# A hybrid encoder block: the first modulation block cut to three k-tiles and summed by two engines

## The chip, the cores and the metric

One core of a Trainium2 chip. The metric is the time of one execution on the device, in microseconds; the number shown is the median of three runs.

## The reference

256 rows `x` of 2048 channels go through one layer. What matters here is its start:

- `mod = silu(c) @ ada_w + ada_b`, with `c` one vector of 2048 and `ada_w` 2048 x 12288, gives shift1, scale1, gate1, shift2, scale2 and gate2 (2048 each).
- `h = RMSNorm(x) * norm1_g * (1 + scale1) + shift1`
- `proj = h @ w_in` (2048 x 9216): columns for a gated MLP (u, v), for attention (q, k, v) and for two gates.

After that come the spatial gating, a banded attention, the merge through `w_out`, a second modulated norm, a router, 32 SwiGLU experts (top 2 of 8 in the best of 4 groups) and a final norm. All is float32.

## The kernel before, in words

A *k-tile* is 128 of the 2048 channels; there are 16. Shift1 and scale1 of a k-tile need 128 columns of two sixths of `ada_w`, over all 2048 rows: 2.1 MB. Only then can that k-tile of `h` be made, and used in products with `w_in`. The kernel therefore walks through `h` in blocks (`BLOCKS`, L40): four blocks of four k-tiles.

`ada_block(k0, n)` (L184) is a generator that does the modulation of one block. It loads 4 chunks of `16 // n` row tiles, each as two DMAs on SP (L192, shift columns and scale columns, 1 MB each), multiplies each row tile by its silu column and adds up on VectorE (L202 the first, L204 the others, 1024 elements wide), transposes the sums on TensorE (L214) and reduces them on VectorE (L217). Three small operations (L220 to L222) make shift and scale, ScalarE applies them (L227), and `h` is kept in two float32r parts, `hh` (L230) and `hl` (L231).

Ahead of the first block: SP issues the ada loads at once; ScalarE's queue issues the small row loads (L158) and the two halves of x (L161); ScalarE squares x (L248) and scales it (L251), TensorE transposes it (L256) and ScalarE copies it out (L261) as `hx`. The spatial weights are transposed there as well (L266).

`run_steps` (L273) does the products of one column group of 1024 with the k-tiles of one block. There are five groups of this kind (`homes`: q, k, v, then the two of the gated MLP), so a block of n k-tiles makes 5n steps. A load brings up to four k-tiles (L108, 2 MB). Per step, ScalarE makes the high half of the weights (L315), VectorE the low half (L316), into two buffers each, and TensorE does 12 products (L289, L290, L291: high by high, low by high, high by low). The products of a step are issued after the preparation of the next. At the end of a group ScalarE copies the result out in the first block (L348), and VectorE adds it in later ones (L350).

The order of the work: `run_steps` takes one item of the next block's `ada_block` after each load and one after each step (`with_ada`). An item is a chunk's pair of loads, one sum, or a piece of the end. All loads of w_in and of ada chunks share one ring of four 16 KB slots, `r0` to `r3` (L100), in the order of the program, and SP issues them in that order: a load waits until its slot's last tenant, four loads before, has been used up. For the last block and for later stages the other four parts of `mod` come the same way (`ada_units`, sums at L427).

```python
for b, n in enumerate(BLOCKS):
    nxt = ada if lastb else ada_block(k0 + n, BLOCKS[b + 1])
    for c0, dst, func in homes:
        run_steps(lh_h, ll_h, win, k0, n, c0, ..., with_ada=nxt, ...)
    ...
    for _ in nxt:
        pass
```

## Time and profile before

| what | value |
|---|---|
| time, median of 3 runs | 1701.71 us (1701.52 to 1702.71) |
| time of the profiled execution | 1703.12 us |
| its span | 1701.3 us, 18241 instructions |
| its mean granted TensorE clock | 0.964 |
| busy share: TensorE, VectorE, ScalarE, GpSimd | 91, 56, 28, 7% |
| mean DMA rate over the span | 368 GB/s |
| chain that ended last | PE 48%, DMA 44%, VectorE 5% |

The shares are averages over three stretches that differ: a front until the first product of `w_in`, a middle of projections and attention, and the experts. In the views, PE is TensorE, PEld its weight loads, DVE VectorE, ACT ScalarE, POOL GpSimd, SP the queue that issues most loads; L204 is line 204 of the kernel. A mean of a group is the time of one instruction; what stands after an arrow is what ended the idle time before it. PEclk is the granted clock as a share of the full one.

### The profile page before, as it was taken

What the parts mean: (1) busy time and instruction counts of PE and PEld (TensorE: products, weight loads), DVE (VectorE), ACT (ScalarE), POOL (GpSimd) and SP (SyncE); (2) the same over time, 40 slices, a digit from 0 to 9 for tenths busy, and PEclk for the clock granted to TensorE, in tenths of its full rate; (3) what the DMA queues carried; (4) which work ended last, traced back from release to release, by engine and by line L of the source; (5) the groups of instructions that cost most, each with busy time, mean ns of one, the idle gap of its engine ahead of it and who ended that gap; (6) DMA issues with size and microseconds to landing.
All of it is one profiled execution on the core that took longest, in us unless ns stands there. A gap on an engine that the chain in (4) does not pass through costs nothing.

```text
span 1701.3 us, 18241 instructions
## 1 busy us (share of the span) xinstructions
PE 1539.8 (91%) x6717; PEld 863.6 (51%) x6717; DVE 951.2 (56%) x1332; ACT 484.4 (28%) x793; POOL 127.2 (7%) x377
## 2 busy tenths in 40 slices
PE   2999999999999999799998989989889898988986
PEld 1777778777887776553333423334333243333332
DVE  5789999998778879733432333323333233332333
ACT  4554345675444345331110111101111011111112
POOL 1000000000000000011100101001010010100101
PEclk8999999999999999799999999999999999999998
DMA  9988997797987876889999999999999999999995
GB/s 359 341 316 332 346 342 298 287 339 285 356 315 295 338 297 235 340 325 418 416 418 418 416 418 415 419 417 417 419 415 418 417 417 418 415 418 417 417 418 196
DMA packets 136766, 625.25 MB, mean 368 GB/s; under 512 B 5592, under 2 KB 7760, under 8 KB 103264
## 3 DMA queue, kind: packets, MB, share of 16 engines
q1 hardware_dynamic: 134240, 614.49, 90.9%
q10 hardware_dynamic: 992, 5.28, 0.8%
q0 software_dynamic: 1440, 4.27, 0.8%
q8 instruction: 55, 0.90, 0.2%
q14 instruction: 39, 0.32, 0.0%
HBM read 621.91 MB, written 2.10 MB: 367 GB/s over the span
## 4 chain that ended last, share of the span: by engine, by line
PE 48%; DMA 44%; DVE 5%; ACT 1%; issue 1%; SPq 0%; POOL 0%; POOLq 0%; DVEq 0%; ACTq 0%
DMA r<-in_w_dram 22%; PE b L1211 11%; PE b L291 10%; PE b L289 10%; DMA E<-in_w_dram 10%; PE b L290 10%; DMA dC<-in_w_dram 10%; DMA r<-in_ada_w_dram 2%; PE b L1236 2%; DVE W L316 1%; PE b L1075 1%; DVE f L427 1%; DVE f L204 0%; PE b L1262 0%; ACT W L315 0%
## 5 line engine op out<-in xcount | busy, mean ns | idle before, releaser
L1264 DVE TENSOR_TENSOR dB<-dB,b 128x512 f32<-128x512 f32 x248 | 153.6, 681 | 326.8 <-PE b L1262 326.8
L315 ACT CAST W<-r 128x1024 fp32r<-128x1024 f32 (+1 forms) x224 | 220.8, 988 | 329.0 <-PE b L290 289.7
L1211 PE MATMUL b<-r,e 128*64 128x512 f32 x1024 | 260.7, 627 | 44.4 <-DMA r<-in_w_dram 44.4
L316 DVE TENSOR_TENSOR W<-r,W 128x1024 fp32r<-128x1024 f32 (+1 forms) x224 | 255.2, 1144 | 62.5 <-ACT W L315 61.3
L289 PE MATMUL b<-W,dC 128*128 128x512 f32 x704 | 284.7, 405 | 5.5 <-ACT dC L230 3.7
L290 PE MATMUL b<-W,dD 128*128 128x512 f32 x704 | 280.1, 398 | 0.0
L291 PE MATMUL b<-W,dC 128*128 128x512 f32 x704 | 267.3, 398 | 2.0 <-DVE W L316 1.9
L1254 ACT CAST f<-f 64x512 fp32r<-64x512 f32 x124 | 76.4, 616 | 590.4 <-DVE dB L1264 430.4
L1211 PEld LDWEIGHTS b<-r,e 128*64 128x64 f32 x1024 | 91.1, 144 | 203.3 <-issue 137.7
L427 DVE SCALAR_TENSOR_TENSOR f<-r,sc,f 128x1024 f32<-128x1024 f32 x123 | 157.3, 1279 | 4.6 <-DMA r<-in_ada_w_dram 3.8
L289 PEld LDWEIGHTS b<-W,dC 128*128 128x128 f32 x704 | 132.8, 189 | 41.1 <-ACT dC L230 4.1
L291 PEld LDWEIGHTS b<-W,dC 128*128 128x128 f32 x704 | 131.5, 188 | 38.6 <-DVE W L316 7.1
L290 PEld LDWEIGHTS b<-W,dD 128*128 128x128 f32 x704 | 132.8, 189 | 30.6 <-issue 0.5
L1211 PE MATMUL b<-E,e 128*64 128x512 f32 x256 | 124.1, 642 | 23.7 <-DMA E<-in_w_dram 23.7
L1211 PE MATMUL b<-dC,e 128*64 128x512 f32 x256 | 118.3, 617 | 19.0 <-DMA dC<-in_w_dram 19.0
L1227 DVE TENSOR_TENSOR f2y<-f2y,b 128x256 f32<-128x256 f32 x32 | 13.5, 422 | 210.2 <-ACT f2y L1226 210.2
L1211 PE MATMUL b<-dD,e 128*64 128x512 f32 x256 | 126.1, 643 | 0.2 <-DMA dD<-in_w_dram 0.2
L1211 PE MATMUL b<-W,e 128*64 128x512 f32 x256 | 120.1, 618 | 0.0
L1236 PE MATMUL b<-r,f2y 128*64 128x512 f32 (+1 forms) x528 | 115.5, 590 | 2.3 <-DVE f2y L1227 2.3
L1255 DVE TENSOR_TENSOR f<-f,f 64x512 fp32r<-64x512 f32 x124 | 85.1, 686 | 26.1 <-ACT f L1254 23.1
L1337 POOL COPY e<-a 128x64 f32 x256 | 69.1, 273 | 195.9 <-PE b L1211 194.4
L1211 PEld LDWEIGHTS b<-E,e 128*64 128x64 f32 x256 | 36.4, 147 | 88.0 <-issue 52.7
(297 smaller groups left out, 1515.8 us busy)
## 6 DMA issues: line engine op xcount, KB each, us to landing
r<-in_w_dram SPq DMA_DIRECT2D x93, 2048.0 KB, 28.1
r<-in_w_in_dram SPq DMA_DIRECT2D x36, 2048.0 KB, 9.2
r<-in_ada_w_dram SPq DMA_DIRECT2D x32, 2048.0 KB, 9.3
W<-in_w_dram SPq DMA_DIRECT2D x24, 2048.0 KB, 28.1
dC<-in_w_dram SPq DMA_DIRECT2D x24, 2048.0 KB, 28.2
dD<-in_w_dram SPq DMA_DIRECT2D x24, 2048.0 KB, 28.2
E<-in_w_dram SPq DMA_DIRECT2D x24, 2048.0 KB, 7.7
r<-in_ada_w_dram SPq DMA_DIRECT2D x32, 1024.0 KB, 10.3
```

The lines of the kernel that those rows point to most:

```text
L289: nc.tensor.matmul(o, a, wh[:, cs], start=(k == k0), stop=False)
L290: nc.tensor.matmul(o, b, wh[:, cs], start=False, stop=False)
L291: nc.tensor.matmul(o, a, wl[:, cs], start=False, stop=close)
L315: nc.scalar.copy(wh, src)
L316: nc.vector.tensor_sub(wl, src, wh.bitcast(F32))
L427: nc.vector.scalar_tensor_tensor(out=acc, in0=rw[:, jj, :], scalar=sc[:, j : j + 1], in1=acc, op0=ALU.mult, op1=ALU.add,)
L1211: nc.tensor.matmul(pab[a * CH : (a + 1) * CH, :], xe[:, 8 * half + j, :], w[:, j // JQ, j % JQ, :], start=(half == 0 and j == 0), stop=(ha ...
L1236: nc.tensor.matmul(po[a * CH : (a + 1) * CH, 0:cw], act[:, j, :], w[:, j, o : o + cw], start=(j == 0), stop=(j == 3),)
L1254: pin(nc.scalar.copy(oh[r, a, :], og[r, b, :]))
L1255: pin(nc.vector.tensor_sub(oh[o, a, :], og[r, b, :], oh[r, a, :].bitcast(F32)))
L1264: pin(nc.vector.tensor_add(xa[:, t, d0 : d0 + 512], xa[:, t, d0 : d0 + 512], pr))
L1337: nc.gpsimd.tensor_copy(xe[:, JQ * q + j, :], Xg[q][j][:, ds(o, CAP)])
```

## The change

- The blocks have 3, 5, 4 and 4 k-tiles.
- The first block has a function of its own, `ada_first`. Its chunks have 4 row tiles of 384 columns. The shift part is summed on TensorE: the silu columns, broadcast to 64 equal columns each, are the stationary operand, and even and odd row tiles go to the two halves of one PSUM bank. The scale part is summed on VectorE as before. Products with one column (`pick`, which takes one row of each half, and `ones`) turn both sums into columns. `hh` comes from one ScalarE operation out of `hx`, and VectorE makes the full value and `hl`.
- The block of five is done as two `ada_block`s of 3 and 2, in one chain, with 2.2 items instead of one at each turn (`hurried`). Chunks have 4 row tiles, or 8 where the block has two k-tiles.
- Both halves of x are issued first on ScalarE's queue; the row loads go to SP, ahead of the ada loads (two of ada_b become one), and `gmlp_b_s` to GpSimd's queue. x is scaled by VectorE; the copies of its transposes alternate between ScalarE and VectorE. The table for Silu is loaded by an early operation, and the squares are held behind the silu of c.
- The transposes of the spatial weights become a side job that runs between steps.

```diff
--- before.py
+++ after.py
@@ -37,7 +37,7 @@
 CW = 1024
 Q = 4
 JQ = D // (Q * P)
-BLOCKS = (4, 4, 4, 4)
+BLOCKS = (3, 5, 4, 4)
 PACE = (0.75, 1.0, 1.0, 0.8, 0.7, 0.7, 0.7)
 OUT_CUTS = ((0, 1024), (1024, 512), (1536, 512))
 
@@ -145,29 +145,31 @@
 
 
     xt = [T([P, D], f"x{t}") for t in range(NT)]
+    for t in range(NT):
+        nc.scalar.dma_start(out=xt[t], in_=x[0, t * P : (t + 1) * P, :])
     rows = T([P, P], "a2")
     nc.vector.memset(rows, 0.0)
     r0 = 0
-    for src in (
-        c[0].rearrange("(j p) -> j p", p=P),
-        norm1_g[0].rearrange("(j p) -> j p", p=P),
-        ada_b[0, 0:D].rearrange("(j p) -> j p", p=P),
-        ada_b[0, D : 2 * D].rearrange("(j p) -> j p", p=P),
-        gmlp_b_s[0],
+    for src, queue in (
+        (c[0].rearrange("(j p) -> j p", p=P), nc.sync),
+        (norm1_g[0].rearrange("(j p) -> j p", p=P), nc.sync),
+        (ada_b[0, 0 : 2 * D].rearrange("(j p) -> j p", p=P), nc.sync),
+        (gmlp_b_s[0], nc.gpsimd),
     ):
-        nc.scalar.dma_start(out=rows[r0 : r0 + src.shape[0], :], in_=src)
+        queue.dma_start(out=rows[r0 : r0 + src.shape[0], :], in_=src)
         r0 += src.shape[0]
-    for t in range(NT):
-        nc.scalar.dma_start(out=xt[t], in_=x[0, t * P : (t + 1) * P, :])
     ws = [T([P, 4, P], "a0"), T([P, 4, P], "a1")]
     for i in range(2):
         nc.gpsimd.dma_start(out=ws[i], in_=gmlp_w_s[0, 4 * i : 4 * i + 4].rearrange("g t s -> t g s"))
+
+    nc.scalar.activation(mhalf[:, 1:2], mhalf[:, 0:1], AF.Silu)
+    nc.vector.memset(mhalf[:, 1:2], -0.5)
     cps = bk.ps()
     nc.tensor.transpose(cps[:, 0:P], rows, ident)
     cols = T([P, P], "cols")
     nc.vector.tensor_copy(cols, cps[:, 0:P])
     sc = T([P, ND], "sc")
-    nc.scalar.activation(sc, cols[:, 0:ND], AF.Silu)
+    sc_made = nc.scalar.activation(sc, cols[:, 0:ND], AF.Silu)
     g1c = cols[:, 16:32]
     b_shift = cols[:, 32:48]
     b_scale = cols[:, 48:64]
@@ -181,11 +183,10 @@
     hl = T([P, ND, S], "dD", F32R)
     accs = Ring(["f0", "f4"])
 
-    def ada_block(k0, n):
+    def ada_pieces(k0, n):
 
         w = n * P
-        acc = accs.sb([P, 2, w])
-        nj = 16 // n
+        nj = 4 if n > 2 else 8
         for j0 in range(0, ND, nj):
             rw = raws.sb([P, nj, 2, w])
             for m in range(2):
@@ -195,6 +196,63 @@
                         0, j0 * P : (j0 + nj) * P, m * D + k0 * P : m * D + k0 * P + w
                     ].rearrange("(j p) n -> p j n", p=P),
                 )
+            yield j0, nj, rw
+
+    def modulation(ks, sums):
+        nc.vector.tensor_add(sh1[:, ks], sums[:, 0, :], b_shift[:, ks])
+        nc.vector.tensor_add(sg1[:, ks], sums[:, 1, :], b_scale[:, ks])
+        nc.vector.scalar_tensor_tensor(
+            out=sg1[:, ks], in0=sg1[:, ks], scalar=1.0, in1=g1c[:, ks], op0=ALU.add, op1=ALU.mult
+        )
+
+    def ada_first(n):
+
+
+        w = n * P
+        scb = T([P, ND, CH], "f4")
+        nc.vector.tensor_copy(scb, sc.unsqueeze(2).to_broadcast([P, ND, CH]))
+        pick = T([P, 1], "pick")
+        nc.vector.tensor_add(pick, ident[:, 0:1], ident[:, CH : CH + 1])
+        pacc = bk.ps()
+        part = T([P, 2, w], "f0")
+        for j0, nj, rw in ada_pieces(0, n):
+            for jj in range(nj):
+                j = j0 + jj
+                i = j % 2
+                nc.tensor.matmul(
+                    pacc[i * CH : (i + 1) * CH, 0:w], scb[:, j, :], rw[:, jj, 0, :],
+                    start=(j < 2), stop=(j >= ND - 2),
+                )
+                if j == 0:
+                    nc.vector.tensor_scalar(part[:, 1, :], rw[:, jj, 1, :], sc[:, 0:1], None, op0=ALU.mult)
+                else:
+                    nc.vector.scalar_tensor_tensor(
+                        out=part[:, 1, :], in0=rw[:, jj, 1, :], scalar=sc[:, j : j + 1], in1=part[:, 1, :],
+                        op0=ALU.mult, op1=ALU.add,
+                    )
+            yield
+        nc.scalar.copy(part[:, 0, :], pacc[:, 0:w])
+        tp = sk.ps()
+        for m, what in enumerate((pick, ones[:, 0:1])):
+            for i in range(n):
+                nc.tensor.matmul(
+                    tp[:, m * n + i : m * n + i + 1], part[:, m, i * P : (i + 1) * P], what,
+                    start=True, stop=True,
+                )
+        modulation(slice(0, n), tp[:, 0 : 2 * n].rearrange("p (a b) -> p a b", a=2))
+        for j in range(n):
+            s, b = sg1[:, j : j + 1], sh1[:, j : j + 1]
+            nc.scalar.activation(hh[:, j, :], hx[:, j, :], AF.Identity, bias=b, scale=s)
+            full = scr[:, j * S : (j + 1) * S]
+            nc.vector.tensor_scalar(full, hx[:, j, :], s, b, op0=ALU.mult, op1=ALU.add)
+            nc.vector.tensor_sub(hl[:, j, :], full, hh[:, j, :].bitcast(F32))
+        yield
+
+    def ada_block(k0, n):
+
+        w = n * P
+        acc = accs.sb([P, 2, w])
+        for j0, nj, rw in ada_pieces(k0, n):
             yield
             for jj in range(nj):
                 j = j0 + jj
@@ -217,11 +275,7 @@
             nc.vector.tensor_reduce(
                 out=sums[:, m, :], in_=tp[:, 0:w].rearrange("p (a b) -> p a b", a=n), axis=AX.X, op=ALU.add
             )
-        nc.vector.tensor_add(sh1[:, ks], sums[:, 0, :], b_shift[:, ks])
-        nc.vector.tensor_add(sg1[:, ks], sums[:, 1, :], b_scale[:, ks])
-        nc.vector.scalar_tensor_tensor(
-            out=sg1[:, ks], in0=sg1[:, ks], scalar=1.0, in1=g1c[:, ks], op0=ALU.add, op1=ALU.mult
-        )
+        modulation(ks, sums)
         yield
         for j in range(k0, k0 + n):
             nc.scalar.activation(
@@ -229,8 +283,24 @@
             )
             nc.scalar.copy(hh[:, j, :], hx[:, j, :])
             nc.vector.tensor_sub(hl[:, j, :], hx[:, j, :], hh[:, j, :].bitcast(F32))
-            if j % 2 == 1:
+            if (j - k0) % 2 == 1 or j == k0 + n - 1:
                 yield
+
+    def ada_of(k0, n):
+
+        if n <= 4:
+            return ada_block(k0, n)
+        return hurried(itertools.chain(ada_block(k0, 3), ada_block(k0 + 3, n - 3)), 2.2)
+
+    def hurried(g, rate):
+        due = 0.0
+        while True:
+            due += rate
+            while due >= 1.0:
+                due -= 1.0
+                if next(g, "end") == "end":
+                    return
+            yield
 
 
     def inv_rms(ss, name):
@@ -241,16 +311,19 @@
         nc.gpsimd.tensor_tensor(out=rs, in0=ve, in1=mhalf, op=ALU.pow)
         return rs
 
-    first = ada_block(0, BLOCKS[0])
+    first = ada_first(BLOCKS[0])
+    next(first)
     ss1 = T([P, NT], "ss1")
     scr = T([P, D], "e2")
-    for t in range(NT):
-        nc.scalar.activation(scr, xt[t], AF.Square, accum_out=ss1[:, t : t + 1])
+    with tc.issue_after(sc_made.ins):
+        for t in range(NT):
+            nc.scalar.activation(scr, xt[t], AF.Square, accum_out=ss1[:, t : t + 1])
     rs1 = inv_rms(ss1, "n1")
     for t in range(NT):
-        nc.scalar.activation(xt[t], xt[t], AF.Copy, scale=rs1[:, t : t + 1])
+        nc.vector.tensor_scalar(xt[t], xt[t], rs1[:, t : t + 1], None, op0=ALU.mult)
+    turned = Ring(["b2", "b3", "b4", "b5", "b6", "b0"])
     for j in range(0, ND, 2):
-        tp = bk.ps()
+        tp = turned.ps()
         for jj in range(2):
             for t in range(NT):
                 nc.tensor.transpose(
@@ -258,16 +331,26 @@
                     xt[t][:, (j + jj) * P : (j + jj + 1) * P],
                     ident,
                 )
-        nc.scalar.copy(hx[:, j : j + 2, :], tp.rearrange("p (a b) -> p a b", a=2))
-    wsT = T([P, 8, P], "f3")
-    for i in range(2):
-        tp = bk.ps()
-        for g in range(4):
-            nc.tensor.transpose(tp[:, g * P : (g + 1) * P], ws[i][:, g, :], ident)
-        nc.scalar.copy(wsT[:, 4 * i : 4 * i + 4, :], tp.rearrange("p (a b) -> p a b", a=4))
-    nc.gpsimd.memset(wsT[CH:P, :, 0:CH], 0.0)
+        tv = tp.rearrange("p (a b) -> p a b", a=2)
+        if j % 4 == 0:
+            nc.scalar.copy(hx[:, j : j + 2, :], tv)
+        else:
+            nc.vector.tensor_copy(hx[:, j : j + 2, :], tv)
     for _ in first:
         pass
+    wsT = T([P, 8, P], "f3")
+
+    def turn_ws():
+        for i in range(2):
+            tp = sk.ps()
+            for g in range(4):
+                nc.tensor.transpose(tp[:, g * P : (g + 1) * P], ws[i][:, g, :], ident)
+            nc.scalar.copy(wsT[:, 4 * i : 4 * i + 4, :], tp.rearrange("p (a b) -> p a b", a=4))
+            yield
+        nc.gpsimd.memset(wsT[CH:P, :, 0:CH], 0.0)
+        yield
+
+    sides.append(turn_ws())
 
 
     def run_steps(lh, ll, w, k0, n, c0, evac, with_ada=None, cw=CW, after=None):
@@ -489,7 +572,7 @@
     k0 = 0
     for b, n in enumerate(BLOCKS):
         lastb = b == len(BLOCKS) - 1
-        nxt = ada if lastb else ada_block(k0 + n, BLOCKS[b + 1])
+        nxt = ada if lastb else ada_of(k0 + n, BLOCKS[b + 1])
         if lastb:
             vecs = T([P, 2, 8, S], "dB")
             lngb = vecs[:, 0].rearrange("p (a b) c -> p a (b c)", a=2)
```

## Rows read from the trace of the kernel before

**Rows 1.** Busy time by stretch, after the count PEclk, DMA share and GB/s.

```profile
0.00:45.00 45.00, 9.27 (x50) 7.57 (x50) 24.69 (x33) 19.30 (x25) 6.91 (x13) 0.87 1.00 362
45.00:90.00 45.00, 45.00 (x182) 35.83 (x182) 34.83 (x33) 22.77 (x31) 0.00 (x0) 0.94 0.92 344
210.00:260.00 50.00, 48.09 (x214) 37.85 (x213) 48.18 (x58) 21.24 (x27) 3.53 (x5) 1.00 0.90 336
820.00:1690.00 870.00, 777.82 (x3308) 299.04 (x3304) 294.10 (x502) 116.39 (x253) 85.20 (x273) 0.96 1.00 409
```

**Rows 2.** Chain of waits, 0 to 46 us: start, duration, what.

```profile
0.77 0.45 SPq L192
...
18.34 14.52 DMA r<-in_ada_w_dram
...
36.94 1.30 DVE f L204
...
45.00 0.79 PE b L289
```

**Rows 3.** Waits of TensorE, 45 to 330 us: total, times, longest.

```profile
PE b L291 <- DVE W L316: 1.7, 3, 1.2
PE b L214 <- DVE f L204: 1.1, 1, 1.1
```

**Rows 4.** Timeline of TensorE and VectorE, 87 to 115 us: start, duration, what.

```profile
87.61 0.39 PE L289 MATMUL b<-W,dC 128*128 128x512 f32 x1
...
90.43 0.39 PE L289 MATMUL b<-W,dC 128*128 128x512 f32 x1
...
114.68 0.69 DVE L350 TENSOR_TENSOR E<-E,b 128x512 f32<-128x512 f32 x1 [1.43 <-PE b L291]
```

**Rows 5.** Timeline of the front, the way of x.

```profile
20.75 3.90 ACT L251 ACTIVATE x<-x,rs_n 128x2048 f32<-128x2048 f32 x2 [3.59 <-POOL rs_n L241]
...
22.81 5.86 PE L256 MATMUL b<-ident,x 128*128 128x128 f32 x32 [13.14 <-ACT x L251]
```

**Rows 6.** Groups of instructions by form, 45 to 105 us: count, busy us, mean ns.

```profile
L316 DVE TENSOR_TENSOR W<-r,W 128x1024 fp32r<-128x1024 f32 x19 | 23.2, 1223 | 11.5 <-ACT W L315 11.5
L315 ACT CAST W<-r 128x1024 fp32r<-128x1024 f32 x19 | 19.9, 1050 | 21.7 <-PE b L290 21.7
L204 DVE SCALAR_TENSOR_TENSOR f<-r,sc,f 128x1024 f32<-128x1024 f32 x15 | 19.2, 1281 | 0.2
...
L227 ACT ACTIVATE dB<-dB,sh,sg 128x256 f32<-128x256 f32 x6 | 3.3, 592 | 0.0
L231 DVE TENSOR_TENSOR dD<-dB,dC 128x256 fp32r<-128x256 f32 x8 | 3.0, 421 | 2.4 <-ACT dC L230 2.4
...
L202 DVE TENSOR_SCALAR f<-r,sc 128x1024 f32<-128x1024 f32 x2 | 1.5, 749 | 0.0
```

**Rows 7.** DMA view of 17 to 33 us, then of 33 to 38 us.

```profile
DMA packets 3030, 6.22 MB, mean 389 GB/s; under 512 B 96, under 2 KB 96, under 8 KB 3030
...
DMA packets 594, 2.02 MB, mean 405 GB/s; under 512 B 16, under 2 KB 16, under 8 KB 594
```

**Rows 8.** Timeline of TensorE, 819 to 827 us.

```profile
819.22 7.09 PE L1211 MATMUL b<-r,e 128*64 128x512 f32 x32
```

**Rows 9.** Timeline of VectorE where it is never idle.

```profile
181.25 1.28 DVE L204 SCALAR_TENSOR_TENSOR f<-r,sc,f 128x1024 f32<-128x1024 f32 x1
182.45 1.22 DVE L316 TENSOR_TENSOR W<-r,W 128x1024 fp32r<-128x1024 f32 x1
183.58 1.28 DVE L204 SCALAR_TENSOR_TENSOR f<-r,sc,f 128x1024 f32<-128x1024 f32 x1
```

**Rows 10.** Timeline, a low half and the load that waits for it.

```profile
54.35 1.23 DVE L316 TENSOR_TENSOR W<-r,W 128x1024 fp32r<-128x1024 f32 x1 [1.92 <-ACT W L315]
...
55.60 0.37 SPq L108 DMA_DIRECT2D r<-in_w_in_dram  x1
```

**Rows 11.** The load of 55.60 us in the view of line L108.

```profile
DMA to landing us min/median/max: 7.6/7.6/7.6
```

## The prediction

> **What bounds the kernel now.** First the busy time by stretch [rows 1]. In 45 to 90 us TensorE is busy without a break, and in 820 to 1690 us the DMA engines are (share 1.00). So the front ends when TensorE gets its first product, the middle runs at TensorE's pace, and the end at the DMA's pace on the expert weights. The weights' first loads wait for slots that the middle frees; what the middle gains or loses moves the end by as much, and I count one to one. The change touches only the first 160 us or so.
>
> The chain of waits of the front [rows 2]: it starts with the issue of the ada loads, follows them to 32.86 us (18.34 + 14.52), then four VectorE sums, the last from 36.94, transposes and the modulation, and the first product starts at 45.0. In the middle, VectorE is the second bound: 48.2 of 50 us in 210 to 260, where TensorE lost 1.9 [rows 1]; TensorE's waits name it too: 1.1 us for the sums of a block (L204, through the transposes L214) and 1.7 for the low halves of the weights (L316) [rows 3]. A step (one k-tile by 1024 columns, 12 products) takes 90.43 - 87.61 = 2.8 us [rows 4]. The first addition of block 2 starts at 114.7 and closes its first four steps [rows 4], so block 2 started at 114.7 - 4 x 2.8 = 103.5, and step 15 of block 1 ended 5 steps before: 89.5. The change has to beat this number.
>
> **The front.** x is not on the chain [rows 2]: its normalisation (3.9 us on ScalarE) and its transposes (5.9 us) run 20.8 to 28.7 [rows 5], ahead of the sums. Moving the scaling to VectorE costs about two 2048-wide multiplications, 1.5 us each by twice L202 less a fixed part (bounds 0.7 and 2.5 each) [rows 6]; it fits under the loads, as do the copies split over two engines, the table load for Silu and the broadcast of the 16 silu columns (below 1.3 us by L204, above 0). Cover for all of this: the ada loads, until 28 us. The row loads now precede the ada loads on SP: three issues of 0.45 us [rows 2], covered because x, issued at once from ScalarE's queue, fills the DMA engines meanwhile. The small row on POOL now leads POOL's queue, ahead of the spatial weights, which nobody needs early.
>
> Loads: in 17 to 33 us the sixteen engines ran 3030 packets of 2053 B in 16 us, 84.5 ns each; in 33 to 38 us 594 of 3401 B in 5 us, 134.7 ns [rows 7]. That is 8 ns plus 0.0372 ns per byte. A three-tile chunk has 1536 B runs, estimate 376 GB/s (389 before); a two-tile one 1024 B, 355; w_in 4096 B, 408. The first chunk before came at 32.9 - 3 x 2.10 MB / 389 = 16.7; with 0.52 MB less in it, 15.3, and three more of 1.57 MB at 4.2 us bring the last to 27.9. Behind it VectorE has four sums of 384 instead of 1024 elements. From L316 and L231, 1.04 ns per element [rows 6], so 1.28 - 0.67 = 0.62 each, 2.5 in all. TensorE's shift products are hidden beside them: 32 of 512 columns took 7.1 us [rows 8], so four of 384 take 0.7 (twice that at half clock). Then three one-column products, three small VectorE operations and one 256-wide ScalarE operation (0.59, [rows 6]): 2 us. Modulated activations at 32.5; the first w_in load lands at 31.7 and its cast and low half take 1.05 + 1.22 [rows 6]. **First product about 33.5, 11.5 us earlier than now.** Were that all, the time would fall by 11.5.
>
> **Block 1 gives most of it back.** It now has 15 steps instead of 20, and under them five k-tiles of ada weights must arrive instead of four. Loads in program order, landing at the rates above: w 31.7, a 35.9, a 40.1, w 43.9, a 48.1, a 52.3, w 56.2, b (two tiles, 2.10 MB) 62.1, w 65.9, b 71.8, w 75.7. Slots do not break this row: each is freed (last low half of a w, last sum of an a or b) before its turn comes. From a landing to the product it feeds go cast and low half, 2.27, less two products that need only the cast (0.47): 1.9 with the hand-over. Steps 1 to 6 end at 33.5 + 2.7 (half clock at the start, as now: 0.94 of 45 us in [rows 1]) + 16.8 = 53, so TensorE waits until 58.1 for w three, then until 67.8, then until 77.6, and step 15 ends at 86.0. VectorE in the same stretch: 16 sums of 768 (0.93 back to back, since starts of L204 lie 1.20 apart where it takes 1.28, [rows 9]) and 16 of 512 (0.67), 13 low halves (1.14), 4 for reductions and the rest: 44 us from 35.9, so 80.3 if never idle; some 3 us idle are free. **Block 2 starts at 86.0 against 89.5: 3.5 us left of 11.5.** Bounds: 82.8 were all ada loads at 389, 89.5 if VectorE loses 10 per cent and the sums come last.
>
> By the Trainium skill, "DMA: Bandwidth & Descriptors", section Where 436 GB/s comes from, loads from HBM are bound at about 358 GB/s per core; 27.3 MB through the last w of block 1 would then land at 79 instead of 75.7, and 3.4 us more would go. This case's rows speak against it: 389 in the loads of the front, and 409 over 870 us [rows 1, 7].
>
> **Block 2's ring of four slots.** Its 5 tiles make two loads per column group, of 4 and of 1. With the two ada chunks of the first group between them, the second group's load of 4 falls on the slot of the first group's: SP waits for the fourth low half of group one. SP is in order; behind this wait stand the third ada chunk and the next load of 1. The row that is nearest: low half at 54.35, load issued 55.60, landed 7.6 us later, with little before it in the queue [rows 10, 11]. Here: start + 5.6 (two steps done) + 2.3 = 7.9, landing 15.5, product 17.4 instead of 14.0. **A stall of 3.4** (bounds 0 and 5). The third group's load waits for the second chunk's last sum; I take 0.7 (0 to 2). Later groups have slack.
>
> **Given back later.** Today a block has 56 us of TensorE for some 57 of VectorE: 20 low halves at 1.14, 20 additions at 0.61 (0.69 in [rows 4] less the same overlap), 16 sums at 1.2 and 3 for the rest. Block 2 of five tiles has 70 for 63 (five low halves more), and the sums for block 3 end in its fourth group. The 1.1 at the boundary goes [rows 3], and of the 1.9 in 210 to 260, where VectorE's backlog ends [rows 1], about 1.0: 2.1 in all (0 to 3). The eight spatial transposes move into block 1, where TensorE waits for loads: 0, or 1 us without that cover.
>
> **Sum.** 3.5 - 3.4 - 0.7 + 2.1 = 1.5 us faster. The profiled execution took 1703.1 around its span of 1701.3, the median is 1701.7; the difference goes against the median: **1700.2**. A measurement of this kernel can tell about 0.2 per cent, 3.4 us, from no change; this is no change.
>
> **Rivals.** (1) *Much of the early start survives* (0.34). The chunk size costs nothing at the DMA, so the last w lands near 72.5 and block 2 starts at 82.8 (6.7 ahead), and the ring's stall is 1 us: 6.7 - 1 + 2.1 = 7.8, so 1694. For it: TensorE never waited in block 1 before. Against: the queue is full there in my sum. (2) *The ring binds every group of block 2* (0.18), each load of 4 coming late by some 3.4 in three groups: -10.2 + 3.5 + 2.1 = 4.6 slower, 1706. It decides once the stalls of block 2 pass 9 us. For it: SP's loads already wait for low halves today; against: after group two the row of slots shifts. (3) *The early start does not happen* (0.06): x, rows and sums collide, first product near 42, DMA behind as computed; block 2 at 88, 1703. (4) *The 358 GB/s bound* (0.02): 3.4 less, 1703.6.
>
> **Chances.** The forecast has 0.40. Its own range, 1697 to 1704, follows from the bounds of its terms; it gives 0.34 to no change, 0.04 to faster, 0.02 to slower. Rival 1 gives 0.32 faster, 0.02 same; 2 gives 0.16 slower, 0.02 same; 3 gives 0.05 and 0.01; 4 is split in halves. Faster 0.36, same 0.44, slower 0.20. The range takes in both main rivals: 1694 to 1706.
>
> **What would show it.** Right: first product at 33 to 35 us; TensorE waiting in block 1 for casts and low halves behind w_in loads; DMA share near 1.00 until 90 us; block 2's first product near 86; one wait of 3 us some 14 us after it. Wrong: TensorE without idle in block 1 (then rival 1), first product after 38 (rival 3), or waits in each group of block 2 (rival 2).

## The result, and the profile after

The changed kernel takes **1720.07 us** (median of 4 runs, 1717.06 to 1720.77) against 1702.21 us of the kernel before, run on the same chip (4 runs): ratio 1.0099, 95% interval 1.0087 to 1.0111. It is slower by 18 us; the forecast was 1700.2, no change, with a range that ended at 1706. The profiled execution took 1719.62 us, its span is 1717.8.

Busy time by stretch, as in [rows 1], and shorter stretches below them:

```profile
0.00:45.00 45.00, 25.44 (x118) 16.56 (x119) 26.15 (x51) 15.13 (x22) 6.82 (x14) 0.92 0.99 347
45.00:90.00 45.00, 35.48 (x127) 26.51 (x126) 37.11 (x47) 21.61 (x32) 0.00 (x0) 0.85 0.97 346
...
820.00:1690.00 870.00, 782.40 (x3308) 304.85 (x3306) 291.64 (x494) 112.22 (x232) 79.77 (x270) 0.96 1.02 416
...
30.00:45.00 15.00, 12.64 (x53) 10.14 (x54) 12.95 (x22) 6.71 (x10) 0.52 (x1) 0.77 1.02 367
45.00:60.00 15.00, 12.25 (x41) 9.11 (x39) 12.50 (x13) 5.79 (x9) 0.00 (x0) 0.77 0.99 355
60.00:75.00 15.00, 12.36 (x44) 9.33 (x42) 10.22 (x18) 7.97 (x14) 0.00 (x0) 0.77 1.06 364
75.00:90.00 15.00, 10.86 (x45) 8.07 (x45) 14.39 (x18) 7.85 (x11) 0.00 (x0) 1.00 0.85 319
...
105.00:120.00 15.00, 10.92 (x38) 7.94 (x37) 14.50 (x15) 3.04 (x3) 0.00 (x0) 0.78 0.94 352
```

TensorE starts earlier, but in 45 to 90 us it now idles for 9.5 us, where it had none, at a granted clock of 0.85 instead of 0.94 [rows 1]. VectorE is not full in that stretch either (37.1 of 45), and the DMA engines are, nearly. The chain of waits over the first 90 us says how this hangs together (compare [rows 2]):

```profile
6.29 13.35 DMA r<-in_ada_w_dram
...
22.30 1.62 DVE x L323 x2
...
25.96 1.80 DVE dB L338 x3
...
32.06 0.63 DVE f L229
32.73 1.46 PE b L238 x6
...
34.54 1.09 PE b L347 x4
...
40.80 1.23 DVE W L399
42.03 0.94 DVE f L262
...
48.14 1.23 DVE W L399
...
54.74 1.23 DVE W L399
55.96 0.94 DVE f L262
...
61.15 1.03 DVE f L262
62.31 0.89 PE b L272 x3
```

In the new kernel L229 is the sum of the scale part, L323 the scaling of x, L338 a copy of its transposes, L238 the one-column products, L347 the spatial transposes, L372 to L374 the products of a step, L398 the cast, L399 the low half, L262 a sum of a later modulation block, L272 its transposes. Before, this chain ran through loads, the last four sums and then TensorE; now, from 42 us on, it runs through five to six modulation sums in a row that stand in VectorE's queue ahead of a low half or of the transposes. (VectorE's timeline of block 1 has 6, 6, 6 and 8 such sums one behind the other, from 41.94, 55.88, 73.93 and 82.25.) The longest waits of TensorE in 30 to 330 us, as in [rows 3]:

```profile
PE b L372 <- ACT W L398: 9.2, 6, 2.5
PE b L374 <- DVE W L399: 4.4, 5, 1.6
PE b L238 <- DVE f L229: 2.0, 1, 2.0
PE b L272 <- DVE f L262: 2.0, 1, 2.0
PE b L524 <- DVE f L510: 1.8, 1, 1.8
```

The largest is for the *cast* (the operation that makes the high half of the weights) on ScalarE, an engine that is half idle. ScalarE's timeline of the changed kernel, at the end of a group and at the late load of block 2:

```profile
58.26 2.69 ACT L431 COPY e<-b 128x512 f32<-128x512 f32 x4 [3.56 <-PE b L374]
60.84 1.99 ACT L398 CAST W<-r 128x1024 fp32r<-128x1024 f32 x2
...
84.53 2.68 ACT L431 COPY x<-b 128x512 f32<-128x512 f32 x4 [3.64 <-PE b L374]
87.11 2.00 ACT L398 CAST W<-r 128x1024 fp32r<-128x1024 f32 x2
...
112.86 2.00 ACT L398 CAST W<-r 128x1024 fp32r<-128x1024 f32 x2 [6.17 <-DMA r<-in_w_in_dram]
```

and of the kernel before at such an end:

```profile
56.07 1.05 ACT L315 CAST W<-r 128x1024 fp32r<-128x1024 f32 x1 [1.75 <-PE b L290]
57.02 1.97 ACT L348 COPY E<-b 128x512 f32<-128x512 f32 x3
58.89 1.05 ACT L315 CAST W<-r 128x1024 fp32r<-128x1024 f32 x1
```

Before, the next group's first cast stands ahead of the copies out of PSUM. Now the four copies come first; they wait for the last product of the old group, and the cast of the new group waits behind them, with its weights landed. The text of this part of the program is the same in both, and has the cast first. So it is the planner, the software that lays out each engine's queue when the kernel is built, that has put them the other way round; what made it do so is not shown here.

To see where the 18 us arise, I number the 80 steps of the four blocks from 0 and take the start of each step's low half (where a row holds several, evenly spaced). Step 15 is the first of block 2 in the changed kernel, step 60 that of the last block in both. "First expert load" is the first expert weight that SP loads.

| us | before | after | distance |
|---|---|---|---|
| step 0 | 40.2 | 35.7 | -4.5 |
| step 15 | 88.8 | 96.8 | +8.0 |
| step 20 | 103.6 | 115.9 | +12.3 |
| step 60 | 220.8 | 231.6 | +10.8 |
| step 80 | 280.2 | 299.2 | +19.0 |
| first expert load | 686.9 | 702.9 | +16.0 |
| end (span) | 1701.3 | 1717.8 | +16.5 |

(A step's first product can start a little before or after its low half; by first products block 2 starts at 97.2 against 89.7, 7.5 late.) So there are **three places**: block 1, the start of block 2, and the last block, which the change does not touch. Three us come back between step 80 and the first expert load; behind it nothing is added.

### The profile page after: what moved, and what is told of

Same layout as the page of the kernel before. It is cut to its first block, busy times and chain, and to the rows that moved or that the text cites. A ratio compares the mean times of both kernels' runs of the same rounds, so it can differ in the third digit from the quotient of the medians.

```text
span 1717.8 us, 18362 instructions
## 1 busy us (share of the span) xinstructions
PE 1556.0 (91%) x6755; PEld 875.7 (51%) x6755; DVE 954.6 (56%) x1363; ACT 477.0 (28%) x785; POOL 126.5 (7%) x378
## 4 chain that ended last, share of the span: by engine, by line
PE 46%; DMA 44%; DVE 6%; ACT 2%; issue 1%; SPq 0%; POOL 0%; POOLq 0%; DVEq 0%; ACTq 0%
DMA r<-in_w_dram 22%; PE b L1294 11%; DMA E<-in_w_dram 10%; PE b L374 10%; DMA dC<-in_w_dram 10%; PE b L372 10%; PE b L373 9%; PE b L1319 2%; DMA r<-in_ada_w_dram 2%; DVE W L399 1%; DVE f L262 1%; PE b L1158 1%; DMA r<-in_w_in_dram 1%; ACT W L398 1%; DVE f L510 1%
## 5 line engine op out<-in xcount | busy, mean ns | idle before, releaser
L1294 PE MATMUL b<-r,e 128*64 128x512 f32 x1024 | 271.2, 644 | 46.1 <-DMA r<-in_w_dram 46.1
L398 ACT CAST W<-r 128x1024 fp32r<-128x1024 f32 (+1 forms) x224 | 220.4, 988 | 332.7 <-PE b L373 307.0
L372 PE MATMUL b<-W,dC 128*128 128x512 f32 x704 | 287.7, 410 | 10.7 <-ACT W L398 10.7
L399 DVE TENSOR_TENSOR W<-r,W 128x1024 fp32r<-128x1024 f32 (+1 forms) x224 | 255.5, 1146 | 70.4 <-ACT W L398 69.6
L374 PE MATMUL b<-W,dC 128*128 128x512 f32 x704 | 272.5, 403 | 4.7 <-DVE W L399 4.5
L372 PEld LDWEIGHTS b<-W,dC 128*128 128x128 f32 x704 | 134.8, 192 | 48.6 <-ACT W L398 14.8
L374 PEld LDWEIGHTS b<-W,dC 128*128 128x128 f32 x704 | 133.2, 191 | 42.9 <-DVE W L399 10.9
L1294 PE MATMUL b<-E,e 128*64 128x512 f32 x256 | 116.0, 607 | 22.0 <-DMA E<-in_w_dram 22.0
L1294 PE MATMUL b<-dD,e 128*64 128x512 f32 x256 | 117.5, 607 | 0.0
L1302 ACT COPY f2x<-b 128x512 f32<-128x512 f32 x32 | 18.8, 586 | 207.5 <-PE b L1294 207.5
## 6 DMA issues: line engine op xcount, KB each, us to landing
W<-in_w_dram SPq DMA_DIRECT2D x24, 2048.0 KB, 28.1
```

The costliest lines, as they stand in the source:

```text
L372: nc.tensor.matmul(o, a, wh[:, cs], start=(k == k0), stop=False)
L374: nc.tensor.matmul(o, a, wl[:, cs], start=False, stop=close)
L398: nc.scalar.copy(wh, src)
L399: nc.vector.tensor_sub(wl, src, wh.bitcast(F32))
L1294: nc.tensor.matmul(pab[a * CH : (a + 1) * CH, :], xe[:, 8 * half + j, :], w[:, j // JQ, j % JQ, :], start=(half == 0 and j == 0), stop=(ha ...
```

## The experiments

Theories: **T1**, the order of VectorE's queue (sums in bursts) holds block 1; **T2**, the landings of the loads hold it; **T3**, the ring of slots delays the first loads of block 2; **T4**, the order of ScalarE's queue (copies ahead of casts) holds block 1. The ratio in each case is to the kernel before on the same chip.

**e1, blocks of four with the new front.** `BLOCKS = (4, 4, 4, 4)`

> The changed kernel with blocks of 4, 4, 4, 4: the new front, no block of five, no hurried sums. Theory 1 (VectorE: the sums of five tiles under fifteen steps stand in bursts ahead of the low halves) and theory 2 (the loads of five tiles under fifteen steps come late) both expect that the early start survives: first product near 38 to 39 us against 45.0 before, no wait of TensorE over 1.5 us in block 1, and a time 5 to 7 us below before, near 1696. If the new front itself is what costs (its moved queues, the spatial transposes), the time is at or above before, 1702 or more.

Measured: 1708.96 us, ratio 1.0038 (1.0025 to 1.0051), not the 1696 that both theories expected. The first product comes at 42.3, not at 38 to 39, and in block 1 TensorE has the same gap of 1.6 us at each end of a group, though the weights were there long before and VectorE is idle for over 3.6 us of each 15:

```profile
45.00:60.00 15.00, 13.38 (x58) 10.48 (x57) 9.15 (x8) 6.90 (x9) 0.00 (x0) 1.00 1.02 391
60.00:75.00 15.00, 13.38 (x58) 10.46 (x57) 11.17 (x10) 6.83 (x9) 0.00 (x0) 1.00 0.93 343
75.00:90.00 15.00, 13.38 (x58) 10.47 (x57) 11.32 (x10) 7.40 (x9) 0.00 (x0) 1.00 0.86 327
```

1.6 us go in each stretch, and this led to T4. Even the front alone, at the old block sizes, is no gain.

**e2, the sums of the five-tile block cut to 64 columns of each part.** `out=acc[:, :, 0:64], in0=rw[:, jj, :, 0:64], ...` A part has 384 or 256 columns there, so this kernel leaves out five sixths or three quarters of each sum; in the trace a sum of 768 elements becomes one of 128 (0.35 us instead of 1.03).

> The changed kernel with the sums of the five-tile block cut to 64 of the columns of each part (the rest of those sums stays zero, so shift and scale of tiles 3 to 7 are left out in part); every load, instruction and order stays. A sum takes some 0.3 us instead of 1.0. Theory 1 expects block 1 to run nearly without waits: first product near 35 as in the changed kernel, block 2 from about 84 instead of 97.5, and a time 10 to 14 us lower, 1706 to 1710. Theory 2 expects block 2 to start within 3 us of the changed kernel's 97.5, since no load comes earlier than its slot and its bytes allow, and a time above 1715.

Measured: 1719.46, ratio 1.0094 (1.0077 to 1.0111). Step 15 moves only from 96.8 to 92.8, where T1 expected 84; by the first product (94.6 for 97.2) and by the time it is what T2 expected. Of the 4.0, 2.4 are left at step 80 and 0.6 in the time. The amount of VectorE's work alone does not hold block 1.

**e3, loads of 3 + 2 tiles in block 2 instead of 4 + 1.** `npc = 3 if n == 5 else 4096 // cw`

> The changed kernel with the five k-tiles of block 2 loaded as 3 and 2 instead of 4 and 1. Theory 3 (the ring of four slots: the load for the second group waits until the first group's load is used up) expects that wait of TensorE in block 2, 108 to 120 us, to go from 4 us and 2 us of half clock to 1 us or less, and the time 4 to 6 us lower, near 1715. If block 2's wait comes from VectorE's queue instead, it stays and the time is within 2 us of the changed kernel's 1720.

Measured: 1715.49, ratio 1.0073 (1.0056 to 1.009), 4.6 less than the changed kernel. The stretch that had 10.92 us of products at a clock of 0.78 now has

```profile
105.00:120.00 15.00, 12.86 (x56) 10.06 (x55) 13.92 (x14) 4.73 (x5) 0.00 (x0) 1.00 0.84 307
```

T3 is right: the late load is gone, and the time falls as expected. But TensorE's idle time there goes from 4.1 to 2.1 us, not to 1 or less: a wait of 2.1 for a low half on VectorE is left, and most of the gain is the clock.

**e4, blocks of 3, 4, 5 and 4.** `BLOCKS = (3, 4, 5, 4)`

> The changed kernel with blocks of 3, 4, 5, 4: block 1 now covers four tiles of ada work instead of five. Theories 1 and 2: block 1 has 1.33 tiles per three steps instead of 1.67, so most of its waits go: block 2 starts near 85, and the stall of the five-tile block's second group moves to block 3. Time 1704 to 1710. If the loss of block 1 does not depend on the five tiles, the time stays at 1718 or more.

Measured: 1724.74, ratio 1.0127 (1.011 to 1.0144). Step 15 comes at 85.3, so a short first block can be fast; but the next two blocks then wait for casts behind late loads (TensorE is busy 10.4 of the 15 us from 90 on, and 9.9 of those from 165 on), and the sum is worse, far above the 1704 to 1710 expected.

**e5, the kernel before with the changed order on ScalarE.** In block 1 the casts of a new group are put behind the copies of the old one:

```diff
+        if k0 == 0 and n == BLOCKS[0]:
+            drain()
...
+                    if "copy" in latest and k0 == 0 and n == BLOCKS[0]:
+                        with tc.issue_after(latest["copy"].ins):
+                            nc.scalar.copy(wh, src)
```

> The kernel before with one thing changed: in block 1 the four copies out of a column group stand ahead of the next group's casts on ScalarE's queue, as they stand in the changed kernel. Theory 4 (the order of ScalarE's queue): the copies wait for the group's last product, so the next cast starts 2.7 us late; TensorE waits 1.6 to 2 us at each of four boundaries of block 1, where it had no wait, and the time rises by 5 to 8 us, to 1708 to 1710. Theory 2 (only the loads' landing counts): no change, since no load moves.

Measured: 1708.2, ratio 1.0034 (1.002 to 1.0049). The kernel before becomes 5.7 us slower, with the picture of e1 in block 1 (13.51, 13.26 and 13.38 us of products in the three stretches of 15): three waits of 1.6 for the cast, and step 15 is 4.2 late. This confirms T4 for block 1 with blocks of four. But the order on ScalarE is not the whole of the 5.7: at step 74 only 2.4 of it are left, and at step 80 it is 9.2 late, with SP's loads of the last block in the changed kernel's order here too (listing at e12).

**e6, e1 with the casts first.** The copies are held back behind the first two casts of the next group:

```diff
+                    if held:
+                        late.append(out_of_psum)
...
+                with tc.issue_after(latest['cast'].ins):
+                    nc.scalar.copy(o, p)
```

> The new front with blocks of 4, 4, 4, 4 (as in the first experiment, 1709) and the first two casts of the next group put ahead of the four copies in block 1. Theory 4: the four waits of 1.6 us at the boundaries go, block 1 keeps the early start, and the time falls by 5 to 7 us to 1702 to 1704, or below 1702 if the early start is then worth what block 1 shows. Theory 2: the time stays within 2 us of 1709.

Measured: 1703.27, ratio 1.0006 (0.9996 to 1.0015), against 1.0038 for e1. The gaps in block 1 are gone:

```profile
45.00:60.00 15.00, 15.00 (x62) 12.03 (x61) 9.52 (x9) 7.09 (x9) 0.00 (x0) 0.93 0.99 370
60.00:75.00 15.00, 14.85 (x64) 11.64 (x63) 12.80 (x11) 7.18 (x9) 0.00 (x0) 1.00 1.03 387
75.00:90.00 15.00, 14.87 (x64) 11.55 (x62) 13.00 (x12) 7.19 (x9) 0.00 (x0) 1.00 0.92 341
```

Step 15 is 3.2 us ahead of the kernel before. But the lead is 2.2 at step 60 and 0.0 at step 80.

**e7, the changed kernel with the casts first.** The edit of e6 at blocks of 3, 5, 4 and 4.

> The changed kernel (1720) with the first two casts of the next group put ahead of the four copies in block 1. Theory 4: the waits for casts in block 1 shrink to those set by landings of loads; block 2 starts 4 to 8 us earlier than 97.5 and the time is 1711 to 1716. What remains above before is then the ring's stall in block 2 (6 us with half clock) and the waits of block 4. Theory 2: the start of block 2 stays within 2 us of 97.5.

Measured: 1719.34, ratio 1.0096 (1.0079 to 1.0112), so no gain, where T4 expected 1711 to 1716: T4 alone falls for this layout. Step 15 comes at 98.0, as T2 expected. TensorE's waits in 45 to 100 us have only changed their name, from the cast (now L412) to the low half (L413) and the sums (L268):

```profile
PE b L380 <- DVE W L413: 5.5, 3, 2.5
PE b L278 <- DVE f L268: 2.1, 2, 1.9
...
PE b L378 <- ACT W L412: 0.6, 1, 0.6
```

**e8, e7 with loads of 3 + 2.** Both edits.

> The same with the five k-tiles of block 2 loaded as 3 and 2. Theories 3 and 4 together: both savings add, 4 us (as the third experiment showed) below the run beside it, 1707 to 1712. If the two share a cause, less than 2 us below.

Measured: 1714.89, ratio 1.0081 (1.0064 to 1.0098), 4.5 below e7, as e3 below the changed kernel, though above the 1707 to 1712 expected, since T4 gave nothing: T3 is independent of T4.

**e9, casts first and narrow sums**, the edits of e7 and e2 at once. The sums are on 64 of a part's 384 or 256 columns, as in e2; the 128 in the expectation is wrong.

> Casts ahead of the copies at the boundaries of block 1 (as in e7) and the sums of the five-tile block on 64 columns of each part instead of 128 (as in e2), both at once. It leaves out the other columns' share of those sums. Each edit alone changed little: e2 moved step 15 from 96.8 to 92.8, e7 not at all (98.0). Theory that the order of VectorE (T1) and the order of ScalarE (T4) each suffice to hold block 1: with both gone TensorE runs nearly without waits, the low half of step 15 comes at 86 to 89, and the time is 1707 to 1713, the waits of the ring in block 2 and in block 4 being left. Rival, the loads' landings hold it (T2): step 15 at 93 or later, TensorE's waits end with the DMA, and the time is 1716 to 1720.

Measured: 1714.93, ratio 1.0078 (1.0061 to 1.0095). Step 15 comes at 87.5, where neither edit alone brought it below 92.8. The time was above what was expected (1707 to 1713), but block 1 is as expected: T1 alone holds all of it (e7), T4 alone some 5 us (e2 against e9). T2 is not what holds it there: the later loads of w_in land at 45.3, 57.8, 67.7 and 79.1, in the changed kernel at 45.4, 57.5, 68.1 and 78.0. But T2 may be the floor beneath: 5.3 us of waits are left in this block 1, the longest 3.1, from 57.5 on, for the cast of the weights that land at 57.8.

**e10, casts first and sums one by one.** Nothing is left out; each sum of the two parts of the five-tile block is queued behind the latest low half:

```diff
+                    behind = len(lows) > 0 and n < 4
+                    with tc.issue_after(lows[-1].ins) if behind else nullcontext():
```

> Casts ahead of the copies (as in e7), and each sum of the five-tile block is queued behind the latest low half, so that no more than one sum or so stands ahead of a low half; no work is left out. If it is the order of VectorE's work (bursts of 5 to 8 sums of 1 us ahead of a low half) that holds block 1 in e7: step 15 at 86 to 91 and 1707 to 1714. If it is the amount of VectorE's work in the block, not its order: step 15 stays within 2 of e7's 98.0 and the time within 2 of 1719.3. A risk that both share: the sums then end late, and the products that need them (shift and scale of the five tiles) wait at the block's end.

Measured: 1716.25, ratio 1.0079 (1.0062 to 1.0096). Step 15 comes at 88.6 instead of 98.0. The low halves (L416) now stand between the sums (L271) in VectorE's timeline:

```profile
61.28 1.22 DVE L416 TENSOR_TENSOR W<-r,W 128x1024 fp32r<-128x1024 f32 x1
62.42 1.01 DVE L271 SCALAR_TENSOR_TENSOR f<-r,sc,f 128x768 f32<-128x768 f32 x1
63.34 1.22 DVE L416 TENSOR_TENSOR W<-r,W 128x1024 fp32r<-128x1024 f32 x1
```

So it is the order, not the amount, of VectorE's work. Of the 9.4 us, 6.7 are left at step 80 and 3.1 in the time, which misses the 1707 to 1714 expected.

**e11, e10 with loads of 3 + 2.**

> e10 with the five-tile loads cut 3 + 2 instead of 4 + 1. The ring theory (T3): 4 to 5 below e10, as e3 was below the changed kernel and e8 below e7. If e10 frees block 1, this comes to 1703 to 1709, no faster than the kernel before by more than 0.2 per cent, since VectorE is nearly always busy in blocks 2 to 4 and a lead is given back there, as in e6. If the stall in block 2 came from a late block 1 alone, no difference to e10 (within 1).

Measured: 1710.99, ratio 1.0048 (1.0031 to 1.0066), 5.3 below e10; it missed the 1703 to 1709 by 2. At step 60 it is 0.6 behind the kernel before, but at step 80 8.6: the last block, again.

**e12, e11 with the last block's loads in program order.** SP's queue there differs from the kernel before, though the program does not. Each load is put behind the one before it (in the listing, from SP's timelines, w is a load of w_in and a one of an ada chunk):

```diff
+        behind = 0 < len(asked) < 13
+        with tc.issue_after(asked[-1]) if behind else nullcontext():
+            d = nc.sync.dma_start(out=t, in_=src)
```

```
SP, last block   before, e12:    w a a w a w a w w a w a
                 after, e5, e11: w a a w a w w a a w a w
```

> e11 with the loads of the last block issued on SP in the order of the program (w, ada, ada, w, ada, w, ada, w, w, ada, as the kernel before has them); in the changed kernel and in e11 the planner put one w load ahead of an ada load and one ada load ahead of a w load there. Theory 5: this order is what costs 4 to 6 us between steps 60 and 80 in every version with blocks of 3, 5, 4 and 4 (the distance to before grows from 0.6 to 8.6 in e11 and from 10.8 to 19.0 in the changed kernel). Then: step 80 at 282 to 285 instead of 288.8, TensorE's wait of 1.8 for a modulation sum in 270 to 300 gone, time 1705 to 1708. Rival: the loss there comes from the first w load of the block, which lands after the group before it has ended; then step 65 stays 3 behind before and step 80 within 2 of 288.8, time within 2 of e11's 1711.

Measured: 1709.52, ratio 1.0038 (1.0024 to 1.0052). Step 80 comes at 284.6 instead of 288.8, and TensorE's wait for a modulation sum (1.8 us, L524 in the list of the changed kernel) is gone. Theory 5 is right for 4.2 us at that step; the time misses the 1705 to 1708 expected: only 1.5 show in it, within the spread of the runs, and 2.8 in the spans. The rival is right for the rest: step 65 is still 3.2 behind before, where step 64 is 0.8 behind.

**e13, e6 with less work for VectorE.** The first sum of a block on ScalarE, the low parts of h on GpSimd:

```diff
-                    nc.vector.tensor_scalar(acc, rw[:, jj], sc[:, 0:1], None, op0=ALU.mult)
+                    nc.scalar.activation(acc, rw[:, jj], AF.Copy, scale=sc[:, 0:1])
-            nc.vector.tensor_sub(hl[:, j, :], ...)
+            nc.gpsimd.tensor_sub(hl[:, j, :], ...)
```

> e6 (blocks of four with the new front and casts first) with less for VectorE in each modulation block: the first of the 16 sums goes to ScalarE (0.75 us in e6) and the four low parts of h to GpSimd (4 x 0.42), together 2.4 us a block, three blocks. If the lead of 3.2 us at step 15 is lost in e6 because VectorE has no idle time in blocks 2 to 4: at least 2 us of it stay until step 80, so step 80 at 276.5 to 278.5 against 280.2, and 1699 to 1701, 0.1 to 0.2 per cent below the kernel before. If it is lost to order and waits instead (a load, the products of the transposes, the new engines being late): step 80 at 279.5 or later and 1702 to 1705.

Measured: 1706.96, ratio 1.0026 (1.0016 to 1.0036), 3.7 above e6 and above both ranges. The lead at step 30 is 4.3, more than e6 has; at step 74 it is 0. TensorE's longest waits in 84 to 285 us:

```profile
PE b L278 <- DVE f L268: 2.9, 3, 1.5
PE b L380 <- DVE W L413: 1.5, 2, 1.0
```

They name the transposes at a block's end, which wait for its last sum, and low halves. So less work for VectorE alone does not keep the lead. Between the first products of steps 30 and 74 it loses 3.9 us, of which 2.2 are such waits (5.5 us of idle against 3.3 before); the rest is other work of TensorE that now falls into this stretch. Which order sets the waits was not tried, and this stays open. Nor do the four blocks hold all of the loss: at step 80 this kernel is 0.8 late, at the first expert load 3.0 and at the end 4.9 (span), and what costs it behind step 80 was not looked into. No version here beats the kernel before.

## Why the prediction was wrong

Term by term, in the distances of the table: the start of block 2 was forecast 3.5 us early and is 8.0 late (11.5 off), the ring adds 4.3 for 4.1, and steps 20 to 80, which were to give 2.1 back, add 6.7 (8.8 off); behind step 80 2.5 come back. That is the 18.0 between -1.5 and the 16.5 of the spans: block 1 and the later blocks failed, about equally. Even all bounds of the prediction taken at their slow end (0, 5, 2 and 0) end at 1709.

**First product: right in kind, 1.9 late.** Forecast 33.5, measured 35.4, 9.6 us earlier than before. The transposes of the spatial weights, costed at "0, or 1 us without that cover", had lost the cover: they stand directly ahead of the first product (34.54, 1.09 us, in the chain). The sums behind the last chunk ended at 32.7, where the forecast's own times (landing at 27.9, 2.5 of sums) give 30.4. The landing was right (28.1), but VectorE still had six sums to do then, not four: the scaling of x and the copies of its transposes, 2.6 and 2.7 us by VectorE's timeline, stood among the sums (L323 and L338 in the chain). The prediction had put them under the loads, at nothing.

**Landings: near.** SP's timeline of the changed kernel, the loads of w_in in block 1:

```profile
32.75 0.37 SPq L108 DMA_DIRECT2D r<-in_w_in_dram  x1
...
48.25 0.37 SPq L108 DMA_DIRECT2D r<-in_w_in_dram  x1
...
57.98 0.39 SPq L108 DMA_DIRECT2D r<-in_w_in_dram  x1
...
71.70 7.31 SPq L108 DMA_DIRECT2D r<-in_w_in_dram  x2
```

By the view of their line they landed 12.7, 9.2, 10.1 and 6.3 us after issue, at 45.4, 57.5, 68.1 and 78.0; forecast 43.9, 56.2, 65.9 and 75.7. The rate with 1.5 KB runs, put at 376 GB/s, is not the reason. The DMA view of 32 to 41 us, where nearly all packets are of that size, and the stretch behind it:

```profile
DMA packets 2043, 3.42 MB, mean 380 GB/s; under 512 B 64, under 2 KB 1896, under 8 KB 2043
...
41.00:45.00 4.00, 4.00 (x21) 3.28 (x20) 3.93 (x4) 1.60 (x3) 0.52 (x1) 1.00 0.93 326
```

They fall behind around two stretches in which the DMA engines were not full: 41 to 45 us, and 54 to 58 with a share of 0.80. The prediction had each slot freed before its turn comes. It was not: SP waited 16.1 us in all, in two waits, for a low half to free an ada load's slot, and issued these loads at 42.05 and 55.99, right behind the low halves that ended at 42.03 and 55.97. That this is the whole reason is not shown.

The bound of 358 GB/s per core of the Trainium skill ("DMA: Bandwidth & Descriptors", section Where 436 GB/s comes from), which the prediction set aside, does not show here either: 380 in this row, 416 GB/s over 870 us in the same kernel, and 391 in 45 to 60 us of e1 are above it.

**The step that failed: "From a landing to the product it feeds go cast and low half, 1.9 with the hand-over."** Weights landed at 68.1 and 78.0, and their first casts started at 75.67 and 87.11, 7.6 and 9.1 later. The step took each queue to serve a piece as soon as its input is there. In the rows above the queues served their pieces in the order in which the planner had laid them out, which was another: copies that wait for TensorE ahead of the cast (T4), five to eight sums ahead of a low half (T1). I had read VectorE as a sum of work ("80.3 if never idle") and ScalarE not at all, since it is idle most of the time. e7, e9 and e10 show that both orders have to go before most of block 1's loss goes, and that with both gone step 15 comes at 87.5 (e9, which leaves out work) or 88.6 (e10) against 88.8 before. By first products block 2 then starts at 89.3 or 90.8 against 89.7: of the forecast lead of 3.5 us at most 0.4 would have been there even then.

**The clock was mis-sized, and some of TensorE's work was missing.** The forecast has 2.7 us of half clock, once, at the start. Now the clock stands at 0.77 in three stretches of 15 us. From the first product to that of block 2, after and before:

```profile
35.39:97.19 61.80, 52.28 (x196) 39.58 (x195) 50.85 (x68) 30.70 (x47) 0.52 (x1) 0.87 0.94 336
...
45.00:89.71 44.71, 44.71 (x180) 35.64 (x181) 34.54 (x32) 22.77 (x31) 0.00 (x0) 0.94 0.92 344
```

Before, the 180 products take 44.7 us without a break, 2.9 of them lost to the lower level of the clock: 41.9 at full clock. After, 9.5 of the 61.8 us are waits. The clock was at its lower level in 35.4 to 38.3, 48.6 to 55.4 and 62.2 to 69.1; TensorE was busy for 15.0 of these 16.6 us and lost half of it, 7.5. The rest of the busy time, 52.3 - 7.5 - 41.9 = 2.9, is transposes (L347, and L272 for the five tiles' sums), which before did not fall into block 1. So 9.6 gained at the first product, less 9.5 of waits, 7.5 - 2.9 of clock and 2.9 of transposes, is 7.4 lost; measured are 7.5. Against the forecast's 42 + 2.7 + 7.8 = 52.5 us (from 33.5 to 86.0), the waits were nearly right in size (1.7 more); their price at the clock (4.8 more) and the transposes (2.9, "0, or 1 us") were not. With the 1.9 of the first product this is the 11.2 us from 86.0 to 97.2.

**Ring of four slots: right in mechanism and place, near in size.** SP issues the load at 105.17, 8.0 us behind block 2's first product (forecast 7.9), when the fourth low half is done, and it lands 7.6 later, as forecast. Forecast were 3.4 + 0.7 = 4.1 us; step 15 to 20 adds 12.3 - 8.0 = 4.3, and e3, e8 and e11 get 4.6, 4.5 and 5.3 back in the time. That these agree so well is in part luck: between the first products of steps 15 and 30 the three gain only 1.7 to 2.7. The wait itself is shorter than the 3.4, and the clock adds the rest; TensorE's timeline at that load:

```profile
113.96 0.80 PE L372 MATMUL b<-W,dC 128*128 128x512 f32 x1 [2.52 <-ACT W L398]
114.55 0.63 PE L373 MATMUL b<-W,dD 128*128 128x512 f32 x1
114.98 0.63 PE L372 MATMUL b<-W,dC 128*128 128x512 f32 x1
```

**Given back later: wrong sign.** I expected 2.1 back from slack in block 2. From step 20 to 60 only 1.5 came, and the last block took 8.2. About half of that is the planner's order of the loads (4.2 in e12); the other part, at the block's first group, is left open.

**The rivals.** None had this case. That TensorE would wait in block 1, that the DMA share would be near 1.00 and that one wait would follow in block 2 was all seen; the end of block 1, 86 forecast, was not (97.2). Rival 2 had the sign, by another mechanism: it put the loss into every group of block 2, and only the first two lose. Rival 3's own terms (1.5 - 4.1 + 2.1) give 1702.2, not 1703; nothing hangs on it.

## What to carry to other kernels

A change of sizes in one part makes the planner order every queue anew, also where the program's text is unchanged; compare the order of each engine's queue, of idle engines and of the loads too, before believing a sum of durations. Where two queues each hold back the same work, removing one may show little: try both together before dropping either. And price a wait of TensorE at its length plus what it does to the granted clock behind it.

## What was not expected of the hardware

A wait of TensorE of two or three us can cost about as much again: it may be followed by the lower of the two clock levels, 1.2 GHz instead of 2.4. In the rows above, products of 512 columns start 0.43 us apart after a wait of 2.52, against 0.23 apart in the same kernel at 95.79 and 96.02; the granted clock of that stretch, 105 to 120, is 0.78. In e3 the one wait there is 2.1 long and the clock stays at 1.00, and so it does in e1 with its waits of 1.6 in three stretches of 15. The length alone does not decide: in block 1 of the changed kernel the lower level also follows a wait of 2.0 (from 60.3 on), shorter than that of e3.
